# Inverse root mean square of 23 norms: GpSimd's power of -0.5 on 128x512 in place of ScalarE's root and VectorE's reciprocal

## The chip, the cores and the metric

The kernel runs on one core of a Trainium2 chip. Time is device time in microseconds (us) of one execution. The engines are TensorE (PE; PEld is its weight load), VectorE (DVE), ScalarE (ACT), GpSimd (POOL) and SyncE (SP), which issues most of the DMAs. Each engine works through its own queue in order and waits on semaphores for the others.

## What is computed

One layer of a streaming encoder on x of 2048 rows by 1024 columns: a mixer (a gated linear recurrence and a gated MLP with a position mixer) and a feed-forward block, each between two RMS norms. The norm is what the change touches:

```
def rmsnorm(x, g):
    y = x * lax.rsqrt(jnp.mean(x * x, axis=-1, keepdims=True) + EPS)
    return y * g

h = rmsnorm(x, g_mix_pre) * (1.0 + sc_m) + sh_m
z = h @ w_in                       # lru_x, lru_gate, gmlp_u, gmlp_v
y = concat([rmsnorm(y_lru, g_lru_out), rmsnorm(y_gmlp, g_gmlp_out)])
x = x + gt_m * rmsnorm(y @ w_out, g_mix_post)
h = rmsnorm(x, g_ffn_pre) * (1.0 + sc_f) + sh_f
up = causal_depthwise_conv(h @ w_up) + b
x = x + gt_f * rmsnorm((gelu(up_g) * up_v) @ w_down, g_ffn_post)
```

## The kernel before

Columns lie on the 128 partitions, rows of x on the free axis, 512 at a time: four chunks c = 0 to 3 in the mixer, two halves C = 0, 1 of 1024 rows (two parts t each) in the feed-forward block. Every float32 matrix product is made of three TensorE matmuls of split operands (hi x hi, hi x lo, lo x hi, `mm3`), 128x512 each. The split (`split`, L136 to L141) is a cast on ScalarE (or GpSimd) and a subtraction on VectorE or GpSimd, so each weight tile and each activation passes through ScalarE and VectorE before TensorE may read it. Weight tiles come from a pool of 8 (four split pairs).

A norm runs in three steps. `SumSq` squares on ScalarE and adds on GpSimd (or VectorE), `rms_split` splits the sums on VectorE, and `rms_bcast` multiplies them with a matrix of 1/D on TensorE (L199), which gives the mean square of each row on all 128 partitions, 128x512 in PSUM. Then r = 1/sqrt(mean + eps) is made in the tile `..._r`, by ScalarE (L202) and VectorE (L203). This is called 23 times, and the tiles are named by their place:

- n1, n2, n3: before the mixer, for chunks 1 to 3 (chunk 0 has code of its own, L725 and L726); read by `build_h` (L253).
- rl0 to rl3 and rg0 to rg3: the two norms in the middle of the mixer; read by `norm_scale` (L530).
- rp0 to rp3: after the mixer's last product; read by `mixer_post` (L604, chunks 0 and 1) and `late_post` (L583, chunks 2 and 3, inside the feed-forward block).
- rq0 to rq3: before the feed-forward block; read by `normed` (L851).
- fr00, fr01, fr10, fr11: after the down-projection of half C, part t; read by `final` (L1112), the last of them at the kernel's end.

In the mixer a chunk's z products (`zblock`: 24 matmuls each) run beside the output products of the chunk before (`mixer_out`: 8 blocks of 24). GpSimd has the odd weight splits (L141), the sums of squares (L219), two products of the recurrence (L380, L503), the copies of split weights to DRAM (L169) and one small power: the variance of the gated MLP's norm, 128x4 (L442). In the feed-forward block the up-projection runs over 24 blocks f; the first two of C = 0 are plain (`up_plain`, 96 matmuls each), the others are made of seven products of 12 matmuls (`up_pair`), whose weights need sums that GpSimd makes (L951, L953, L956, L959) in C = 0 and for the first two f of C = 1. The down-projection runs over 24 f with 24 matmuls each.

The order of the work on each engine is not the order of the code: a scheduler replays the program with priorities (`high_priority`) and estimated durations, and each engine's queue is fixed by it. So a change of one operation moves others too.

Of the kernel before, what the change touches and what calls it, by code (L numbers as in the profile page):

```python
# [12 lines left out]
AF = mybir.ActivationFunctionType  # L13
ALU = mybir.AluOpType

P = 128
# [24 lines left out]
def block_kernel(ctx: ExitStack, tc: tile.TileContext, xt, cols, rows, wada, wada_r, win_k, win_s, win_v, wgate, wsp, wout, wup, wdown, out):  # L41
# [12 lines left out]
    vec, act, pool, pe, sync = nc.vector, nc.scalar, nc.gpsimd, nc.tensor, nc.sync  # L54
# [15 lines left out]
    def bank(name):  # L70

        return banks[0].tile([P, 512], F32, tag="pf", name=name) if banks else psum(name)[:, 0]
# [52 lines left out]
    epst = const.tile([P, 1], F32, name="epst")  # L125
    vec.memset(epst, EPS)
    mhalf = const.tile([P, 4], F32, name="mhalf")
# [67 lines left out]
    def rms_bcast(shl, scale, name, tag="r2", bufs=2, n=512):  # L195

        pt = bank(f"{name}_m")
        for q in range(2):
            pe.matmul(out=pt[:, :n], lhsT=onesD, rhs=shl[:, q, :n], start=(q == 0), stop=(q == 1))  # L199
        r = rp.tile([P, 512], F32, tag="r", name=f"{name}_r")  # L200
        with tc.high_priority(offset=100):
            act.activation(out=r[:, :n], in_=pt[:, :n], func=AF.Sqrt, scale=scale, bias=epst)  # L202
            vec.reciprocal(out=r[:, :n], in_=r[:, :n])  # L203
        return r

    class SumSq:
# [27 lines left out]
    def x_rms(c, late=2):  # L234
        q = SumSq(f"n{c}")
        for j in range(4):
            q.add(load_x(xt, c, j, f"xq{c}"))
            yield
        yield
        hl = q.done()  # L240
        yield from wait(late)
        rx[c] = rms_bcast(hl, 1.0, f"n{c}", "rr", 4)
# [271 lines left out]
    def norm_scale(c, late=2):  # L514

        qs = []
        for tiles, name in zip(HU[c], (f"rl{c}", f"rg{c}")):
            qs.append(SumSq(name))
            for t in tiles:
                qs[-1].add(t)  # L520
            yield
        hls = [q.done() for q in qs]
        yield from wait(late)
        rs = [rms_bcast(hl, 2.0, f"r{n}{c}") for n, hl in zip("lg", hls)]
        yield
        for tiles, gname, r in zip(HU[c], ("g_lru_out", "g_gmlp_out"), rs):
            for j in range(2):
                for b in range(2):
                    t = tiles[j][:, b]
                    vec.scalar_tensor_tensor(out=t, in0=t, scalar=col(gname, 2 * j + b), in1=r, op0=ALU.mult, op1=ALU.mult)  # L530
                yield
# [37 lines left out]
    def late_rms(c, q):  # L569
        hl = q.done()  # L570
        yield
        rlate[c] = rms_bcast(hl, 1.0, f"rp{c}")
# [655 lines left out]
```

## Time and profile before

| | |
|---|---|
| Median of 3 runs | 2222.09 us (2219.21 to 2222.97) |
| The profiled execution's own time | 2222.2 us |
| Its span, first to last instruction | 2220.4 us |
| Mean granted TensorE clock | 0.971 |
| Busy: TensorE, VectorE, ScalarE, GpSimd | 2072.0, 1435.9, 928.8, 424.8 us |

The stages of the profiled execution: chunk 0 of the mixer until about 95 us, the other chunks until about 700 us, up-projection of the first half until about 1200, its down-projections until about 1460, then the same for the second half, and the end at 2220. A row of the profile names the line of the kernel, the engine, the operation, and what it writes and reads; a line can be that of a helper that many callers share, so the names of the tiles tell the place.

### The profile page before, as it was taken

What the parts mean: (1) busy time and instruction counts of PE and PEld (TensorE: products, weight loads), DVE (VectorE), ACT (ScalarE), POOL (GpSimd) and SP (SyncE); (2) the same over time, 40 slices, a digit from 0 to 9 for tenths busy, and PEclk for the clock granted to TensorE, in tenths of its full rate; (3) what the DMA queues carried; (4) which work ended last, traced back from release to release, by engine and by line L of the source; (5) the groups of instructions that cost most, each with busy time, mean ns of one, the idle gap of its engine ahead of it and who ended that gap; (6) DMA issues with size and microseconds to landing.
All of it is one profiled execution on the core that took longest, in us unless ns stands there. A gap on an engine that the chain in (4) does not pass through costs nothing.

```text
span 2220.4 us, 24098 instructions
## 1 busy us (share of the span) xinstructions
PE 2072.0 (93%) x9032; PEld 1700.7 (77%) x9032; DVE 1435.9 (65%) x1598; ACT 928.8 (42%) x1154; POOL 424.8 (19%) x248
## 2 busy tenths in 40 slices
PE   5898969999998998799999999989999999999995
PEld 4686858888877876588888888868888888888883
DVE  7788789795766887898777437474444444533634
ACT  3472733534635544355555344343233332422422
POOL 4454243234203332443320000020000000000000
PEclk9999989999999999899999999999999999999997
DMA  8587568587674887877775546537666666444541
GB/s 315 187 311 286 193 242 291 206 287 256 225 268 164 305 314 265 311 264 276 271 291 189 181 134 215 173 120 286 220 221 224 220 223 221 145 159 149 212 148 60
DMA packets 157748, 501.14 MB, mean 226 GB/s; under 512 B 15296, under 2 KB 15424, under 8 KB 157632
## 3 DMA queue, kind: packets, MB, share of 16 engines
q1 hardware_dynamic: 149568, 470.25, 59.9%
q0 software_dynamic: 6912, 25.17, 2.9%
q10 hardware_dynamic: 1152, 4.19, 0.5%
q8 instruction: 71, 1.16, 0.2%
q14 instruction: 45, 0.37, 0.1%
HBM read 343.31 MB, written 156.24 MB: 225 GB/s over the span
## 4 chain that ended last, share of the span: by engine, by line
PE 73%; DVE 14%; ACT 4%; DMA 4%; issue 4%; POOL 1%; SPq 0%; DVEq 0%; ACTq 0%; POOLq 0%
PE dn L177 8%; PE dn L178 8%; PE dn L179 8%; PE upa L973 7%; PE upa L972 7%; PE upa L971 7%; PE upc L973 3%; PE upc L972 3%; PE upc L971 3%; PE upb L973 2%; PE upb L971 2%; PE upb L972 2%; PE lg L177 1%; PE lg L178 1%; PE lg L179 1%
## 5 line engine op out<-in xcount | busy, mean ns | idle before, releaser
L177 PE MATMUL dn<-gh,wd_h 128*128 128x512 f32 x768 | 297.0, 390 | 2.9 <-ACT fr_r L202 1.6
L178 PE MATMUL dn<-gl,wd_h 128*128 128x512 f32 x768 | 296.6, 389 | 0.0
L141 DVE TENSOR_TENSOR wd_l<-wd_r,wd_h 128x1024 fp32r<-128x1024 f32 x96 | 118.0, 1230 | 231.9 <-ACT wd_h L136 216.1
L179 PE MATMUL dn<-gh,wd_l 128*128 128x512 f32 x768 | 265.0, 389 | 0.0
L136 ACT CAST wd_h<-wd_r 128x1024 fp32r<-128x1024 f32 x96 | 101.2, 1056 | 286.8 <-PE dn L178 276.1
L918 DVE SCALAR_TENSOR_TENSOR a<-Rg,prm,a 128x1023 f32<-128x1023 f32 x92 | 132.4, 1439 | 126.9 <-ACT a L916 126.7
L177 PEld LDWEIGHTS dn<-gh,wd_h 128*128 128x128 f32 x768 | 144.2, 188 | 35.4 <-ACT wd_h L136 3.0
L179 PEld LDWEIGHTS dn<-gh,wd_l 128*128 128x128 f32 x768 | 144.1, 188 | 29.8
L178 PEld LDWEIGHTS dn<-gl,wd_h 128*128 128x128 f32 x768 | 144.2, 188 | 29.8
L918 DVE SCALAR_TENSOR_TENSOR a<-Rv,prm,a 128x1023 f32<-128x1023 f32 x92 | 121.9, 1325 | 38.7 <-ACT a L916 38.5
L951 POOL TENSOR_TENSOR wt<-wuv,wug 128x512 f32<-128x512 f32 x24 | 39.3, 1637 | 523.7 <-DMA wuv<-in_wup_dram 411.7
L916 ACT ACTIVATE a<-Rv,prm 128x1024 f32<-128x1024 f32 x46 | 57.2, 1244 | 133.3 <-DVE Rv L1020 132.6
L136 ACT CAST wt<-wt 128x512 fp32r<-128x512 f32 x72 | 44.7, 622 | 113.3 <-PE upa L973 39.5
L141 DVE TENSOR_TENSOR wt<-wt,wt 128x512 fp32r<-128x512 f32 x72 | 62.7, 873 | 24.0 <-ACT wt L136 23.8
L976 ACT ACTIVATE a<-a 128x1024 f32<-128x1024 f32 x48 | 50.9, 1061 | 53.7 <-DVE a L923 31.9
L1020 DVE TENSOR_TENSOR Rv<-upa,m 128x512 f32<-128x512 f32 x46 | 31.6, 687 | 58.3 <-PE upa L973 58.3
L141 DVE TENSOR_TENSOR gl<-gr,gh 128x1024 fp32r<-128x1024 f32 x48 | 58.5, 1218 | 12.5 <-PE upa L973 6.3
L977 DVE TENSOR_TENSOR a<-a,a 128x1024 f32<-128x1024 f32 x48 | 58.8, 1225 | 2.5 <-ACT a L976 2.5
L916 ACT ACTIVATE a<-Rg,prm 128x1024 f32<-128x1024 f32 x46 | 57.2, 1243 | 4.4 <-DVE a L918 3.2
L136 ACT CAST gh<-gr 128x1024 fp32r<-128x1024 f32 x48 | 50.8, 1058 | 13.3 <-DMA gr<-gd 6.1
L1024 ACT COPY Rg<-upa 128x512 f32<-128x512 f32 x46 | 26.8, 584 | 69.7 <-PE upa L973 69.7
L959 POOL TENSOR_TENSOR wt<-wug,wt 128x512 f32<-128x512 f32 x24 | 39.9, 1662 | 82.4 <-DVE wt L141 55.5
(583 smaller groups left out, 5738.5 us busy)
## 6 DMA issues: line engine op xcount, KB each, us to landing
wd_r<-in_wdown_dram SPq DMA_DIRECT2D x96, 512.0 KB, 4.4
wkd<-wt SPq DMA_DIRECT2D x88, 512.0 KB, 4.0
wkd<-w SPq DMA_DIRECT2D x66, 512.0 KB, 3.7
w<-wkd SPq DMA_DIRECT2D x66, 512.0 KB, 4.3
gd<-a SPq DMA_DIRECT2D x48, 512.0 KB, 3.9
gr<-gd SPq DMA_DIRECT2D x48, 512.0 KB, 3.5
wrt<-wkd SPq DMA_DIRECT2D x44, 512.0 KB, 4.3
wt<-wkd SPq DMA_DIRECT2D x44, 512.0 KB, 4.6
```

The lines of the kernel that those rows point to most:

```text
L136: act.copy(out=hi, in_=src)
L141: (leng or vec).tensor_tensor(out=lo, in0=src, in1=hi.bitcast(F32), op=ALU.subtract)
L177: pe.matmul(out=out, lhsT=wh, rhs=mh, start=first, stop=False)
L178: pe.matmul(out=out, lhsT=wh, rhs=ml, start=False, stop=False)
L179: pe.matmul(out=out, lhsT=wl, rhs=mh, start=False, stop=last)
L916: act.activation(out=a, in_=R, func=AF.Identity, scale=w[2], bias=col("ffn_conv_b", blk))
L918: vec.scalar_tensor_tensor(out=a[:, s:], in0=R[:, :FT - s], scalar=w[t], in1=a[:, s:], op0=ALU.mult, op1=ALU.add)
L971: pe.matmul(out=pt, lhsT=wh, rhs=mh, start=first and not more and k == 0, stop=False, skip_group_check=more)
L972: pe.matmul(out=pt, lhsT=wh, rhs=ml, start=False, stop=False, skip_group_check=more)
L973: pe.matmul(out=pt, lhsT=wl, rhs=mh, start=False, stop=last and k == 3, skip_group_check=more)
L976: act.activation(out=g, in_=g, func=AF.Gelu_apprx_tanh)
L977: vec.tensor_tensor(out=g, in0=g, in1=v, op=ALU.mult)
```

## The change

`rms_bcast` makes r in another way. ScalarE no longer takes the root of the mean square plus eps but only adds eps (the Identity function with the same scale and bias), and leaves the sum in r in SBUF. GpSimd then raises r to the power of -0.5, in place; the exponent is the constant column `mhalf`, read with a step of zero over the 512 columns. VectorE's reciprocal is gone. All 23 calls change; the code of chunk 0 (L725, L726) keeps its root and reciprocal.

```
         with tc.high_priority(offset=100):
-            act.activation(out=r[:, :n], in_=pt[:, :n], func=AF.Sqrt, scale=scale, bias=epst)
-            vec.reciprocal(out=r[:, :n], in_=r[:, :n])
+            act.activation(out=r[:, :n], in_=pt[:, :n], func=AF.Identity, scale=scale, bias=epst)
+            pool.tensor_tensor(out=r[:, :n], in0=r[:, :n], in1=mhalf[:, 0:1].broadcast_to([P, n]), op=ALU.pow)
         return r
```

ScalarE's queue has 42 loads of a function table before and 25 after: the 11 at L202 are gone, and six on balance that served other lines.

VectorE's queue at the end of chunk 0, where n1_r is made and read (the win tiles are weight splits of chunk 1, x is the input to be scaled; - is before, + after):

```order
 L141 TENSOR_TENSOR win_10_l<-win_10_r,win_10_h 128x1024
 L444 SCALAR_TENSOR_TENSOR nm_891<-bag_879,rv_880 128x4
-L203 RECIPROCAL n_r<-n_r 128x512
+L141 TENSOR_TENSOR win_0_l<-win_0_r,win_0_h 128x1024
+L141 TENSOR_TENSOR win_2_l<-win_2_r,win_2_h 128x1024
 L253 SCALAR_TENSOR_TENSOR x_0_960<-x_0_960,sm,n_r 128x512 x2
 L253 SCALAR_TENSOR_TENSOR x_1_1007<-x_1_1007,sm,n_r 128x512 x2
```

The reciprocal is gone, two weight splits of the next chunk have moved ahead of the readers of n_r, and the readers now wait for GpSimd.

GpSimd's queue in chunk 1 (rl and rg are the two norms of chunk 0, rv the small power, xc the recurrence's input):

```order
+L219 TENSOR_TENSOR n_s_1182<-n_s_1182,n_s_1297 128x1024
 L169 DMA kept_s_1_1549<-win_5_l 128x1024
+L219 TENSOR_TENSOR n_s_1182<-n_s_1182,n_s_1352 128x1024
+L203 TENSOR_TENSOR rl_r<-rl_r,mhalf 128x512
+L203 TENSOR_TENSOR rg_r<-rg_r,mhalf 128x512
 L442 TENSOR_TENSOR rv_1696<-rv_1696,mhalf 128x4
 L380 TENSOR_TENSOR xc_0_1140<-xc_0_1140,i_0_1653 128x1024
```

Two powers stand back to back ahead of the small power and of the recurrence's product, and the sums for n2 have moved behind a weight split.

GpSimd's queue in the up-projection of C = 0 (wt_4 and wt_5 are weights of f = 4 and 5, rp_r the norm of chunk 3):

```order
 L951 TENSOR_TENSOR wt_4_5379<-wuv_4_5376,wug_4_5375 128x512
 L953 TENSOR_TENSOR wt_4_5379<-wuv_4_5376,wt_4_5379 128x512
 L956 TENSOR_TENSOR wuv_4_5376<-wuv_4_5376 128x512
-L959 TENSOR_TENSOR wt_3_5216<-wug_3_5212,wt_3_5216 128x512
 L959 TENSOR_TENSOR wt_4_5379<-wug_4_5375,wt_4_5379 128x512
+L203 TENSOR_TENSOR rp_r<-rp_r,mhalf 128x512
 L951 TENSOR_TENSOR wt_5_5552<-wuv_5_5549,wug_5_5548 128x512
```

A power stands between the weights of f = 4 and those of f = 5. In the same way rp2 stands ahead of the weights of f = 2, rq2 of f = 9 and rq3 of f = 13. On VectorE the readers of fr00 and fr10 (L1112) stand behind the weight splits of 18 blocks f of the next down-projection in the new order, where they came right after the reciprocal; those of fr01 and fr11 follow directly in both.

## Rows read from the trace of the kernel before

**Rows 1.** The page: busy time by engine, and the ended-last chain by engine.

```profile
PE 2072.0 (93%) x9032; PEld 1700.7 (77%) x9032; DVE 1435.9 (65%) x1598; ACT 928.8 (42%) x1154; POOL 424.8 (19%) x248
...
PE 73%; DVE 14%; ACT 4%; DMA 4%; issue 4%; POOL 1%; SPq 0%; DVEq 0%; ACTq 0%; POOLq 0%
```

**Rows 2.** Busy time by stretch: start:end, length, busy us of PE to POOL.

```profile
core 0: us, PE busy (x) PEld busy (x) DVE busy (x) ACT busy (x) POOL busy (x), PEclk, DMA share, GB/s
120.00:770.00 650.00, 607.04 (x2701) 500.59 (x2700) 501.61 (x529) 318.64 (x384) 221.94 (x118) 0.97 0.70 251
...
1330.00:2220.00 890.00, 849.76 (x3724) 699.27 (x3722) 430.62 (x495) 293.83 (x352) 14.66 (x8) 0.98 0.55 187
```

**Rows 3.** Lines 202 and 203: ns min/median/max; the last is L203's stretch.

```profile
L202 ACT ACT_TABLE_LOAD  x11: 1283/1283/1283, 127.2 to 2064.4; - x11
...
L203 DVE RECIPROCAL n_r<-n_r x3: 3339/3344/3352, 129.3 to 422.3; 128x512 f32<-128x512 f32 x3
...
120.00:770.00 650.00, 56.56 (x17) 0.97 0.70 251
```

**Rows 4.** Chain that ended last, in order of time: start us, us, what.

```profile
127.24 1.28 ACT L202
129.26 3.36 DVE n_r L203
...
260.88 1.22 DVE n_r L203
...
422.34 3.26 DVE n_r L203
...
427.88 3.26 DVE rq_r L203
...
1472.26 3.35 DVE fr_r L203
...
2199.47 3.36 DVE fr_r L203
```

**Rows 5.** GpSimd's plain additions: line 951 (ns min/median/max) and one of L219.

```profile
L951 POOL TENSOR_TENSOR wt<-wuv,wug x24: 1262/1661/2686, 710.0 to 1485.1; 128x512 f32<-128x512 f32 x24
...
187.19 2.40 POOL L219 TENSOR_TENSOR rg_s<-rg_s,rg_s 128x1024 f32<-128x1024 f32 x1 [1.10 <-ACT rg_s L215]
```

**Rows 6.** GpSimd's small power, line 442, and VectorE beside one of them.

```profile
L442 POOL TENSOR_TENSOR rv<-rv,mhalf x4: 1037/1192/2051, 124.8 to 539.1; 128x4 f32<-128x4 f32 x4
...
539.06 1.19 POOL L442 TENSOR_TENSOR rv<-rv,mhalf 128x4 f32<-128x4 f32 x1 [2.10 <-DVE rv L441]
...
539.40 0.69 DVE L141 TENSOR_TENSOR rq_hl<-rq_s,rq_hl 128x512 fp32r<-128x512 f32 x1
```

**Rows 7.** Timeline of the end, from the last product on.

```profile
2198.75 0.69 ACT L202 ACTIVATE fr_r<-fr_m,epst 128x512 f32<-128x512 f32 x1 [3.58 <-PE fr_m L199]
2199.47 3.35 DVE L203 RECIPROCAL fr_r<-fr_r 128x512 f32<-128x512 f32 x1 [1.61 <-ACT fr_r L202]
2202.86 5.39 DVE L1112 SCALAR_TENSOR_TENSOR fo<-fo,gf,fr_r 128x512 f32<-128x512 f32 x8
```

**Rows 8.** TensorE around its longest wait in the mixer, and the clock there.

```profile
289.10 0.39 PE L177 MATMUL o<-rg0h,wout_h 128*128 128x512 f32 x1
289.32 0.39 PE L178 MATMUL o<-rg0l,wout_h 128*128 128x512 f32 x1
...
308.94 0.77 PE L177 MATMUL o<-rl0h,wout_h 128*128 128x512 f32 x1 [18.13 <-DVE modc L285]
309.50 0.63 PE L178 MATMUL o<-rl0l,wout_h 128*128 128x512 f32 x1
309.93 0.63 PE L179 MATMUL o<-rl0h,wout_l 128*128 128x512 f32 x1
...
298.00:300.00 2.00, 0.00 (x0) 0.00 (x0) 2.00 (x4) 2.00 (x3) 0.00 (x0) 0.50 1.03 422
```

**Rows 9.** VectorE's L366 beside the addition at 187.19 us, and later alone.

```profile
187.39 2.21 DVE L366 SCALAR_TENSOR_TENSOR xc<-tails,prm,xc 128x2 f32<-128x2 f32 x1
...
193.93 0.20 DVE L366 SCALAR_TENSOR_TENSOR xc<-tails,prm,xc 128x2 f32<-128x2 f32 x1
```

## The prediction

> **What bounds the kernel now.** The first view is the page's busy time by engine: TensorE is busy for 93% of the span and VectorE for 65%, GpSimd for 19% [rows 1]. The second is the chain that ended last: 73% of it is TensorE and 14% VectorE [rows 1]. So time is lost only where TensorE stands still. The third view, busy time by stretch, says where VectorE is the next to matter: in the mixer, from 120 to 770 us, TensorE is busy for 607.0 of 650 us and VectorE for 501.6 [rows 2]; after 1330 us VectorE is busy for less than half of the time. The work that the change touches is small. The 23 reciprocals take 3.34 us each, 76.9 us of VectorE in all, and the roots bring 11 table loads of 1.283 us onto ScalarE [rows 3]. In the chain in order of time only six reciprocals stand, with 3.36, 1.22, 3.26, 3.26, 3.35 and 3.36 us, 17.8 us together, and one table load of 1.28 us [rows 4]. That is all that the removed work costs directly: 19.1 us.
>
> **What is removed.** The root becomes an Identity of the same shape on ScalarE, so its 0.69 us stays. The table loads in the order of the program fall from 42 to 25, 17 x 1.283 = 21.8 us of an engine that is busy for 42%, of which 1.28 us is on the chain. The reciprocals go from VectorE, 56.6 us of them from the mixer [rows 3].
>
> **What is added, and its price.** GpSimd gets 23 powers on 128x512, and no row shows one of that size. The nearest rows bound it from both sides. A plain two-input GpSimd operation takes 1.262 us at best on 128x512 and 2.40 on 128x1024 [rows 5], which is (2.40 - 1.262) / 512 = 2.22 ns an element and 0.12 us to start. That is the lower end: if a power costs no more than an add, p = 1.3 us. The one row with a power is that of 128x4: 1.037, 1.192 (median), 2.051 us [rows 6]. At 4 elements an add by the line above would take 0.13 us, so about 0.91 us is the power's own. If all of it is a start cost, p = 1.26 + 0.91 = 2.2 us. If all of it is paid element by element, it is 0.91 / 4 = 0.2275 us each, and p = 0.12 + 512 x 0.2275 = 117 us; from the median instead of the lowest call it would be 137. The ends are far apart. The row of the same operation is the nearer one, and with four elements it already costs seven times the addition, so I go by it. But its first call took 1.0 us more than its shortest for the same four elements, so a call has a start cost that comes and goes; I leave a third of the 0.91 us to that and take two thirds by element: 0.152 us each, p = 0.12 + 0.30 + 512 x 0.152 = **78 us**, an estimate between the ends of 1.3 and 137.
>
> [...]
>
> **Where the powers land.** Each r is read by VectorE, and VectorE and GpSimd work in order, so what stands behind is held as well. From the order of the program, shown ahead, I sort the 23.
>
> Fourteen stand in the mixer with their VectorE reader next in line: n1 to n3, the four rl, the four rg, rp0, rp1 and rq1. While VectorE waits for them, the weight splits and gate work behind it wait, and GpSimd's own share of the splits, L380 and L503 stand behind the power. What VectorE can catch up is its idle time in the mixer, 650 - 501.6 = 148.4 us, and the 17 reciprocals that it no longer runs there, 56.6 us [rows 2, 3], 205 us together. Cost: 14 x 78 - 205 = 887 us. The floor from GpSimd's own load is not far below: it is busy for 221.9 us there [rows 2], and with these fourteen, rp2 and rq0 it would have 221.9 + 16 x 78 = 1470 us of work for a stretch of 650, 820 more.
>
> Two are read with nothing between: fr01, whose reciprocal is on the chain at 1472.26 us, and fr11 at 2199.47, after which only the last scaling and the stores remain [rows 4, 7]. Each costs 78 - 3.35 = 75 us, 150 together.
>
> Three (rp3, rq2, rq3) have late readers, but on GpSimd the sums that make the up-projection's weights stand behind them (L951). TensorE has one block of f in hand, 84 matmuls at 0.227 us from start to start [rows 8], 19 us. Cost: 3 x (78 - 19) = 177 us.
>
> rp2 has the two plain blocks as cover, and rq0 one mixer_out: 192 matmuls either way, 43.6 us. Cost: 2 x (78 - 44) = 68 us.
>
> fr00 and fr10 are read 18 blocks of f later, 18 x 24 x 0.227 = 98 us: nothing.
>
> Each stall also slows TensorE's clock for a while: after the wait of 18.13 us at 308.94 the granted clock is 0.50, the level of 1.2 GHz, and ten matmuls start 0.43 us apart in place of 0.227 [rows 8], 2.0 us. Over 21 stalls, 42 us.
>
> The sum is 887 + 150 + 177 + 68 + 42 = 1324 us. Against the profiled execution's own 2222.2 us (span 2220.4, and the median of the runs is 2222.09, so no shift is needed) that is **3546 us**. For any p over 44 us the same sum reads 1908 + 21 p.
>
> **The rivals.**
>
> *The power's excess is a start cost* (p about 2.2 us). Then the six reciprocals and the table load on the chain, 19.1 us, become six powers, 13.2 us: 2216 us. If VectorE's freed 76.9 us is also felt in the mixer, up to its 43 us of TensorE idle, it could fall to 2179; I put it at 2212. This is the side of faster. The price decides: replaced one for one on the chain a power pays below 19.1 / 6 = 3.2 us, and from about 205 / 14 = 15 us on the mixer's slack is used up. For it: every other GpSimd row has a start near 0.1 us and a small slope. Against it: 0.91 us for four elements is more than any start in the trace. In this case the moved instructions also decide a few us either way; the TensorE wait of 18.13 us for the modulation [rows 8] has other blocks around it in the new order.
>
> *Everything is by element* (p = 117): 1908 + 21 x 117 = 4365 us; with p = 137 it is 4785. For it: the only row with the operation, taken as it stands. Against it: the first call's extra us.
>
> *A shorter element* (p between 18 and 45, say 30): 14 x 30 - 205 + 2 x 27 + 3 x 11 + 42 = 344, so 2566 us. It needs a loop that works on several elements at once, which four elements would not show. At p = 15 only 5 + 23 and some of the clock are left, about 2270.
>
> *The port.* A VectorE operation with two SBUF inputs is held by a GpSimd operation: L366 on 128x2 takes 0.20 us alone and 2.21 us when it starts beside an add of 2.40 us, and both end together [rows 9]. If a power holds VectorE for its whole length, it stops where nobody reads r, too: fr00 and fr10 cost 78 - 11 (two blocks of weights in hand) each, 134 us, and the covers of the five others shrink to 11, another 2 x 33 + 3 x 8 = 90: 3770 us, and 4667 with p = 117 (4365 + 2 x 106 + 90). Against it: beside the power at 539.06 a VectorE operation with two SBUF inputs ran at its usual 0.69 us [rows 6]; but four elements are read at once.
>
> The Trainium skill, SBUF — State Buffer, section Who interferes with whom, calls that pair of ports an exclusive lock, held for the whole instruction by whoever starts first. The rows of L366 agree; the row at 539.40 does not show it. By the rule the time is this rival's.
>
> **How the numbers follow.** The chance of p between 45 and 100 (2850 to 4010 us, port or not) is 0.42; of over 100 (4010 and up) 0.27; of 18 to 45 (2330 to 2850) 0.17; of 10 to 18 (2240 to 2330) 0.04; of a start cost 0.10, of which 0.07 is faster and 0.03 within 0.2%. The likeliest gives 3546 us. The range from 2330 to 4800 leaves out the start cost, the 10 to 18, and some 0.04 above for the port with p over 117, 0.18 in all. A measurement of this kernel can tell about 0.2%, 4.4 us, from no change. Faster by more: 0.07; within: 0.03; slower by more: 0.90.
>
> **What would show it.** The row of L203 on GpSimd gives p at once; GpSimd's busy time should be near 425 + 23 p, 2200 us. In the waits VectorE should wait for GpSimd's n, rl, rg, rp and rq (L253, L530, L604) for some 60 us each time, TensorE's granted clock should fall in the mixer, and the tail should grow by 75 us between the last Identity and L1112. If L203 reads under 3 us there, the first rival holds and all of the sum falls. If VectorE's two-input operations last as long as a power, the port is the better account. If p is near 78 and the time is under 3000, the cover was misjudged.

## The result

The changed kernel takes 3619.28 us (median of 4 runs, 3613.97 to 3620.29), beside 2222.53 us for the kernel before on the same chip (4 runs, 2219.21 to 2224.73). The ratio is 1.628, with a 95% interval of 1.6254 to 1.631. The profiled execution took 3619.97 us with a span of 3618.2, so its rows stand for the median.

The first view is the page of the kernel after: busy time by engine, and the chain that ended last by engine. They answer to [rows 1].

```profile
PE 2105.9 (58%) x9032; PEld 1720.8 (48%) x9032; DVE 1397.0 (39%) x1575; ACT 906.3 (25%) x1137; POOL 2296.0 (63%) x271
...
PE 30%; issue 16%; POOL 9%; POOLq 2%; DVE 2%; DMA 1%; ACT 1%; SPq 0%; DVEq 0%; ACTq 0%
```

TensorE's work is the same 9032 matmuls and only 34 us longer, but it is now 58% of the span in place of 93%. GpSimd went from 424.8 to 2296.0 us. No engine is full; the time is lost in waits between engines. The shares of the chain in this page add up to about 60%, so I read the waits and the stretches instead.

The price stands in the rows of the powers. The groups are those of line 203 and of the small power of line 442 (ns min/median/max, first and last start):

```profile
L203 POOL TENSOR_TENSOR rl_r<-rl_r,mhalf x4: 81929/81939/81950, 291.1 to 1521.8; 128x512 f32<-128x512 f32 x4
L203 POOL TENSOR_TENSOR rg_r<-rg_r,mhalf x4: 81914/81917/81936, 373.0 to 1603.7; 128x512 f32<-128x512 f32 x4
L203 POOL TENSOR_TENSOR fr_r<-fr_r,mhalf x4: 81917/81918/82545, 2551.8 to 3518.9; 128x512 f32<-128x512 f32 x4
...
L442 POOL TENSOR_TENSOR rv<-rv,mhalf x4: 999/1314/2052, 124.5 to 1399.3; 128x4 f32<-128x4 f32 x4
```

A power on 128x512 takes 81.9 us, nearly the same each time, where the reciprocal took 3.34 [rows 3].

Who waits is in the list of waits of the kernel after: engine and line, what released it, us in total, times, the longest.

```profile
DVE uu L530 <- POOL rg_r L203: 292.8, 4, 75.5
PE rp_m L199 <- DVE rp_hl L140: 287.1, 2, 144.8
DVE r L530 <- POOL rl_r L203: 280.9, 4, 79.8
PE upc L971 <- ACT wt L136: 195.9, 4, 85.0
ACT rq_s L215 <- POOL oo L605: 192.2, 7, 86.3
DVE x L253 <- POOL n_r L203: 177.7, 3, 63.1
DVE oo L604 <- POOL rp_r L203: 158.9, 2, 80.1
ACT wt L136 <- POOL wt L951: 155.3, 5, 78.4
DVE fo L1112 <- POOL fr_r L203: 150.8, 2, 83.6
```

Five of these rows are readers of r on VectorE (L530 twice, L253, L604, L1112). ScalarE's wait for L951 is of the other kind: plain additions on GpSimd that came late because a power stood ahead of them. (L605 adds to what L604 makes, so it is late with its reader.) The 195.9 us of TensorE are the end of that second chain: power, sum of weights (L951), cast on ScalarE (L136), product. TensorE's two longest waits (L199, 287.1 us) are for the split sums of squares of a later norm (rp_hl); at the second of them GpSimd makes the last of these sums at 1276.98 us, right behind the powers rl and rg.

By stretch (start:end, length, busy us and counts of PE, PEld, DVE, ACT, POOL, the granted clock) the kernel after reads as below; the cuts are the first matmul of the up-projection and the first of the down-projection.

```profile
120.00:1750.00 1630.00, 551.06 (x2320) 445.83 (x2319) 417.80 (x450) 267.78 (x320) 1452.49 (x116) 0.66 0.25 88
1750.00:2407.00 657.00, 480.39 (x2043) 392.64 (x2043) 398.70 (x440) 238.16 (x342) 448.35 (x101) 0.85 0.56 210
2407.00:3618.00 1211.00, 992.01 (x4341) 816.68 (x4339) 493.93 (x558) 352.15 (x420) 340.95 (x12) 0.91 0.48 156
```

The same cuts in the kernel before:

```profile
120.00:682.00 562.00, 519.04 (x2321) 427.92 (x2319) 433.26 (x464) 276.19 (x327) 191.17 (x102) 0.96 0.71 253
682.00:1186.00 504.00, 475.95 (x2029) 388.39 (x2030) 412.05 (x445) 249.24 (x349) 164.96 (x96) 0.97 0.75 274
1186.00:2220.00 1034.00, 993.09 (x4354) 817.59 (x4353) 504.84 (x563) 355.66 (x423) 14.66 (x8) 0.98 0.54 183
```

So 1068 of the 1398 us of span come in the mixer, 153 in the up-projection of the first half and 177 in the rest. In the mixer TensorE does the same 2320 matmuls in 551 us in place of 519: 32 us are the lower clock (0.66 granted on the mean), the rest is standing still.

The end, in the timeline of the kernel after (start, us, engine, line), answers to [rows 7]:

```profile
3518.09 0.69 ACT L202 ACTIVATE fr_r<-fr_m,epst 128x512 f32<-128x512 f32 x1 [3.58 <-PE fr_m L199]
3518.85 81.92 POOL L203 TENSOR_TENSOR fr_r<-fr_r,mhalf 128x512 f32<-128x512 f32 x1 [48.14 <-ACT fr_r L202]
3600.80 5.39 DVE L1112 SCALAR_TENSOR_TENSOR fo<-fo,gf,fr_r 128x512 f32<-128x512 f32 x8 [83.60 <-POOL fr_r L203]
```

From the start of the Identity to that of L1112 it is 82.7 us where it was 4.1: fr11 costs 78.6 us with nothing to hide it.

### The profile page after: what moved, and what is told of

Its sections match the earlier page's. It is cut to its first block, busy times and chain, and to the rows that moved or that the text cites. A ratio compares the mean times of both kernels' runs of the same rounds, so it can differ in the third digit from the quotient of the medians.

```text
span 3618.2 us, 24077 instructions
## 1 busy us (share of the span) xinstructions
PE 2105.9 (58%) x9032; PEld 1720.8 (48%) x9032; DVE 1397.0 (39%) x1575; ACT 906.3 (25%) x1137; POOL 2296.0 (63%) x271
## 4 chain that ended last, share of the span: by engine, by line
PE 30%; issue 16%; POOL 9%; POOLq 2%; DVE 2%; DMA 1%; ACT 1%; SPq 0%; DVEq 0%; ACTq 0%
POOL fr_r L203 5%; PE upa L971 4%; PE upa L972 4%; PE upa L973 4%; PE dn L177 2%; POOLq L1223 2%; POOL rg_r L203 2%; PE dn L178 2%; PE dn L179 2%; PE upc L973 2%; PE upc L971 2%; PE upc L972 2%; PE upb L971 1%; PE upb L972 1%; PE upb L973 1%
## 5 line engine op out<-in xcount | busy, mean ns | idle before, releaser
L203 POOL TENSOR_TENSOR fr_r<-fr_r,mhalf 128x512 f32<-128x512 f32 x4 | 328.3, 82074 | 812.4 <-ACT fr_r L202 812.4
L203 POOL TENSOR_TENSOR rp_r<-rp_r,mhalf 128x512 f32<-128x512 f32 x4 | 328.7, 82178 | 42.1 <-ACT rp_r L202 42.1
L203 POOL TENSOR_TENSOR rl_r<-rl_r,mhalf 128x512 f32<-128x512 f32 x4 | 327.8, 81939 | 30.0 <-ACT rl_r L202 30.0
L203 POOL TENSOR_TENSOR rq_r<-rq_r,mhalf 128x512 f32<-128x512 f32 x4 | 329.3, 82327 | 15.5 <-ACT rq_r L202 15.5
L203 POOL TENSOR_TENSOR rg_r<-rg_r,mhalf 128x512 f32<-128x512 f32 x4 | 327.7, 81921 | 0.0
L203 POOL TENSOR_TENSOR n_r<-n_r,mhalf 128x512 f32<-128x512 f32 x3 | 246.8, 82261 | 9.6 <-ACT n_r L202 9.6
L136 ACT CAST wd_h<-wd_r 128x1024 fp32r<-128x1024 f32 x96 | 101.2, 1056 | 308.8 <-PE dn L178 300.5
L177 PE MATMUL g<-xch,ghi 128*128 128x512 f32 x32 | 16.3, 508 | 266.4 <-ACT gg L409 135.5
L199 PE MATMUL rp_m<-rp_hl,onesD 128*128 128x512 f32 x8 | 3.7, 487 | 287.1 <-DVE rp_hl L140 287.1
L530 DVE SCALAR_TENSOR_TENSOR uu<-uu,prm,rg_r 128x512 f32<-128x512 f32 x16 | 27.6, 1785 | 292.8 <-POOL rg_r L203 292.8
L951 POOL TENSOR_TENSOR wt<-wuv,wug 128x512 f32<-128x512 f32 x24 | 38.3, 1599 | 159.3 <-DMA wuv<-in_wup_dram 98.9
L199 PEld LDWEIGHTS rp_m<-rp_hl,onesD 128*128 128x128 f32 x8 | 1.7, 213 | 288.1 <-issue 145.2
L177 PEld LDWEIGHTS g<-xch,ghi 128*128 128x128 f32 x32 | 7.7, 240 | 270.1 <-ACT gg L409 136.7
```

Of the source, the lines that this page charges most:

```text
L136: act.copy(out=hi, in_=src)
L177: pe.matmul(out=out, lhsT=wh, rhs=mh, start=first, stop=False)
L203: pool.tensor_tensor(out=r[:, :n], in0=r[:, :n], in1=mhalf[:, 0:1].broadcast_to([P, n]), op=ALU.pow)
L951: pool.tensor_tensor(out=t1, in0=b12, in1=b11, op=ALU.subtract)
```

## The experiments

All comparisons below are with the kernel before on the same chip (2221 to 2224 us). A time given with one number is one run. The theory of the prediction is that a power is paid by element, and that VectorE's wait for it, with what stands behind the power on GpSimd, carries the loss. The rivals were another price, GpSimd's load alone, readers alone, and the port.

**Half of the columns.** The power does 256 of the 512 columns (edit against the kernel after; three dots stand for what is left out here).

```
-            act.activation(out=r[:, :n], in_=pt[:, :n], func=AF.Identity, scale=scale, bias=epst)
-            pool.tensor_tensor(out=r[:, :n], in0=r[:, :n], ..., op=ALU.pow)
+            m = n // 2
+            act.activation(out=r[:, :m], in_=pt[:, :m], func=AF.Identity, scale=scale, bias=epst)
+            act.activation(out=r[:, m:n], in_=pt[:, m:n], func=AF.Identity, scale=0.0, bias=one)
+            pool.tensor_tensor(out=r[:, :m], in0=r[:, :m], ..., op=ALU.pow)
```

> The changed kernel with the power on the first 256 of the 512 columns alone; the other 256 are set to 1 by a second ScalarE operation (the inverse root of half of the rows is left out). By element, the power takes 256 x 0.16 = 41.0 us and the sum of the prediction for that price, 14 x 41 - 205 + 2 x 37.6 + 3 x 22 + 42, gives 552 us on top of 2222: 2774 us. If a third of the price were a start cost, the power would take 27 + 27 = 55 us and the time would be 3060 us.

It took 2771.42 us, as the price by element had it (2774). The rows of its powers:

```profile
L205 POOL TENSOR_TENSOR rg_r<-rg_r,mhalf x4: 41110/41114/41603, 291.5 to 1023.6; 128x256 f32<-128x256 f32 x4
L205 POOL TENSOR_TENSOR fr_r<-fr_r,mhalf x4: 41115/41116/41959, 1810.8 to 2711.2; 128x256 f32<-128x256 f32 x4
```

Between 256 and 512 columns the medians of rg give (81.917 - 41.114) / 256 = 0.1594 us for each column, and 81.917 - 512 x 0.1594 = 0.3 us are left as a start. The price is by element. With four elements that line gives 0.95 us, and the shortest call of L442 took 1.00: the small power lies on the same line, though one width could not tell its slope from its start.

**A product in place of the power.** The same instructions on the same engines, but GpSimd multiplies (edit against the kernel after).

```
-            act.activation(out=r[:, :n], in_=pt[:, :n], func=AF.Identity, scale=scale, bias=epst)
-            pool.tensor_tensor(out=r[:, :n], ..., op=ALU.pow)
+            act.activation(out=r[:, :n], in_=pt[:, :n], func=AF.Identity, scale=0.0, bias=one)
+            pool.tensor_tensor(out=r[:, :n], ..., op=ALU.mult)
```

> The changed kernel with the price of the power taken away and everything else kept: GpSimd multiplies the 128x512 tile by the same constant column in place of raising it to the power, and ScalarE's Identity has scale 0 and bias 1, so r is a constant and not the inverse root (that part of the computation is left out). If the price of the power (81.9 us each) is the whole of the loss, as the prediction's sum has it, the time falls to between 2185 and 2222 us, since the six reciprocals and one table load on the chain (19.1 us) become six multiplications of about 1.6 us (9.6 us). Rival: the new order of the work on the engines costs something by itself; then the time stays above 2240 us.

It took 2219.92 us (12 runs; 17 of before, 2222.08), ratio 0.9985 (0.9975 to 0.9995). The products took 1.03 to 2.7 us each. So the way over GpSimd costs nothing as long as its operation is short, and the loss comes with the price of the power. The order of the queues is not that of the change, though. Here VectorE's readers of fr00 follow right behind the product (start at 1334.8 us, the product's at 1333.1); in the change they start 86 us after the power does (2637.6 and 2551.8), behind other work and without a wait for it. The run takes away the price and the order that goes with it together; no run has that order with a cheap operation, so what the order alone costs is not shown. At the price of a product this way of making r brings some 2 us, though 19.1 us of root and reciprocal stood on the chain [rows 4].

**The power on four columns.** Each row of x needs only one power. Here the sums are made with rows on partitions, 128x4, raised there, spread over a diagonal and copied to all partitions by one more product (the eight small matmuls are left out here).

```
...
+            act.activation(out=rc, in_=pt.rearrange(...)[:, :, 0], func=AF.Identity, ..., bias=epsc)
+            pool.tensor_tensor(out=rc, in0=rc, in1=mhalf, op=ALU.pow)
+            vec.tensor_tensor(out=r..., in0=ident..., in1=rc..., op=ALU.mult)
+            pe.matmul(out=pt, lhsT=onesD.bitcast(F32), rhs=r, start=True, stop=True)
+            act.copy(out=r, in_=pt)
```

> The power on 128x4 in place of 128x512: the row sums are made with the rows on the partitions (eight small matmuls), the power takes four elements per partition, and a product of a diagonal tile with a constant matrix on TensorE spreads r over the partitions again. It computes the reference. If the price goes by the elements of one partition, the power takes about 1.0 us as in the small one of the gated MLP's norm, VectorE has 0.7 us in place of 3.34 for each norm, and the time is 2200 to 2222 us, at or a little below the kernel before. If the power has a price that does not depend on the elements, or if the longer chain of small steps is on the path 23 times (some 2 us each), the time is 2240 us or more.

It took 2254.93 us (4 runs), ratio 1.0149 (1.0136 to 1.0162). The power is cheap again (1.25 us on the mean of the 23), and 1397 us of the change's loss are down to 33. TensorE's busy time is 2114.2 us beside 2072.0: 184 more matmuls, 42 us on the engine that bounds the kernel. That accounts for the 33 by size, and TensorE's idle time did not grow (140.7 us of the span, 148.4 before), so the longer chain of small steps is not what costs; no run takes these matmuls away alone.

**Powers that nobody reads.** Root and reciprocal make r; behind them GpSimd raises a copy that ScalarE makes.

```
+            act.activation(out=r[:, :n], in_=pt[:, :n], func=AF.Sqrt, scale=scale, bias=epst)
+            vec.reciprocal(out=r[:, :n], in_=r[:, :n])
+            d = sp.tile([P, 512], F32, tag="rd", name=f"{name}_d")
+            act.activation(out=d[:, :n], in_=pt[:, :n], func=AF.Identity, ...)
+            pool.tensor_tensor(out=d[:, :n], in0=d[:, :n], ..., op=ALU.pow)
```

> ScalarE's root and VectorE's reciprocal of the kernel before make r, and the 23 powers run beside them on a tile that nobody reads. Nobody waits for a power now; only what is queued behind one on GpSimd still does. If the loss comes from readers that wait for r, the time falls to 2222 to 2320 us. If it comes from GpSimd's load (16 powers of 81.9 us and 222 us of other work in a mixer of 650 us, and the weights' sums behind rp3, rq2 and rq3), the mixer still needs some 880 us more and the up-projection some 150 to 190, and the time is 3200 to 3350 us.

It took 3490.34 us: with no reader at all, 1268 of the 1397 us are still there, more than either theory had. But the copy has one buffer, so ScalarE waited for each power before it could write the next (some 310 us in all). The next run takes that away.

**The same without ScalarE's copy.** The power reads r itself and writes the tile that nobody reads.

```
-            act.activation(out=d[:, :n], in_=pt[:, :n], func=AF.Identity, ...)
-            pool.tensor_tensor(out=d[:, :n], in0=d[:, :n], ..., op=ALU.pow)
+            pool.tensor_tensor(out=d[:, :n], in0=r[:, :n], ..., op=ALU.pow)
```

> ScalarE's root and VectorE's reciprocal make r as in the kernel before, and every reader takes that r; behind each, GpSimd raises r to -0.5 into a tile that nobody reads, and ScalarE writes nothing for it. It differs from the earlier run with unread powers in that ScalarE no longer waits for the one tile that the powers worked in. If what is queued behind the powers on GpSimd carries most of the loss, the mixer can't end before GpSimd has gone through its 16 powers and the work among them: 16 x 82 + 222 = 1534 us before the up-projection, against 682 before, so the time stays between 3050 and 3490 us. If most of the earlier run's loss was ScalarE's wait for that tile, the time falls to 2222 to 2600 us.

It took 3542.4 us, above the range given: ScalarE's wait had not been the cause. Its waits:

```profile
DVE rp_s L225 <- POOL rp_s L221: 430.7, 3, 144.5
PE rp_m L199 <- DVE rp_hl L140: 420.1, 3, 145.7
DVE rl_s L225 <- POOL rl_s L221: 212.8, 3, 79.5
```

What is late here are the sums of squares of the next norm (rp_s, rl_s; L219 of the kernel before): additions of 2.4 us that stand behind one or two powers on GpSimd. TensorE then waits for them to make the next norm.

**Only the four powers of the feed-forward's norms.**

```
+            if name[:2] == "fr":
                 (Identity and power)
+            else:
+                (root and reciprocal)
```

> Only the four powers of the feed-forward's norms (fr00, fr01, fr10, fr11) are done by GpSimd, the other 19 as before. If fr01 and fr11 each stand on the path with 82 - 3 = 79 us and fr00 and fr10 are covered, as the prediction's sum has it: 2222 + 158 = 2380 us (2365 to 2400). If only the end of the kernel waits (fr11), because fr01 is covered too: 2300 us. If all four stand on the path: 2538 us.

It took 2401.12 us, 180 above the kernel before, 21 above the sum of two powers and just outside the range given. Its first matmuls of up- and down-projection stand where they did (682.4 and 1186.5 us); all of it comes behind them. The timeline around fr01, GpSimd's rows first, then TensorE's:

```profile
1498.00 81.92 POOL L204 TENSOR_TENSOR fr_r<-fr_r,mhalf 128x512 f32<-128x512 f32 x1 [23.09 <-ACT fr_r L203]
1587.69 2.18 POOL L955 TENSOR_TENSOR wt<-wuv,wug 128x512 f32<-128x512 f32 x1 [7.78 <-DVE fo L1117]
...
1481.04 0.80 PE L975 MATMUL upa<-h_10h,w 128*128 128x512 f32 x1 [24.82 <-ACT fo L1079]
...
1505.17 0.39 PE L977 MATMUL upa<-h_11h,wt 128*128 128x512 f32 x1
1590.57 0.79 PE L975 MATMUL upc<-hs_10h,wt 128*128 128x512 f32 x1 [85.01 <-ACT wt L136]
```

At the start of the power TensorE had 7 us of products in hand. Then it waited for the power (to 1579.9), for VectorE's readers of r (the next sum of weights, L951 of the kernel before, waits 7.78 us more for fo), and for sum and cast: 85.0 us. In the kernel before, the wait at this place was 8.8 us long, behind the same readers, so fr01 costs 76:

```profile
1488.00 0.80 PE L971 MATMUL upc<-hs_10h,wt 128*128 128x512 f32 x1 [8.78 <-ACT wt L136]
```

Another 25 us come ahead of fr01's power: TensorE waits 24.8 us at 1481.04 for the first product of the second half, which came without a wait before. They go back to fr00. Its readers run at 1420.2 us in place of 1341.5, its stores follow them, and on SyncE the load of the second half's x stands behind the last of these stores. SyncE's rows before and, below the dots, in this run:

```profile
1372.62 0.38 SPq L1114 DMA_DIRECT2D out_dram<-fo  x1
1373.09 0.42 SPq L228 DMA_DIRECT2D xf<-x2d  x1
...
1452.01 0.38 SPq L1118 DMA_DIRECT2D out_dram<-fo  x1
1452.48 11.86 SPq L232 DMA_DIRECT2D xf<-x2d  x2
```

ScalarE's part in the norm of that x comes late with it, and behind it in ScalarE's queue stands the copy (L1079) that TensorE waits for. The same wait is 25.6 us long in the change. This chain is read from the trace; no run has fr00 alone. The last matmul of the up-projection starts 100 us later than before (2033.0 beside 1932.6), and the rest is the end. By this reading fr00 costs 25 us, fr01 76, fr10 nothing and fr11 79.

**Only rp2, rp3, rq2 and rq3**, the four beside the up-projection, by the same kind of condition:

```
+            if name in ("rp2", "rp3", "rq2", "rq3"):
```

> Only the four powers whose waits the prediction put beside the up-projection (rp2, rp3, rq2, rq3) are done by GpSimd, the other 19 as before. The prediction's sum has 82 - 44 = 38 us for rp2 and 82 - 19 = 63 us for each of the other three, 227 us in all: 2449 us. In the changed kernel the stretch from the first matmul of the up-projection to the first of the down-projection grew by 153 us only: 2375 us, if that holds with the mixer undisturbed. If the weights of the up-projection don't wait behind the powers at all: 2222 to 2270 us.

It took 2368.43 us, 146 above the kernel before and near the 2375 taken from the changed kernel's own stretch. The four first matmuls behind the powers (TensorE's timeline; in brackets the wait):

```profile
731.62 0.79 PE L975 MATMUL upc<-hs_00h,wt 128*128 128x512 f32 x1 [6.43 <-ACT wt L136]
852.30 0.80 PE L975 MATMUL upc<-hs_00h,wt 128*128 128x512 f32 x1 [57.91 <-ACT wt L136]
996.07 0.80 PE L975 MATMUL upc<-hs_00h,wt 128*128 128x512 f32 x1 [48.07 <-ACT wt L136]
1122.47 0.80 PE L975 MATMUL upa<-h_00h,wt 128*128 128x512 f32 x1 [49.93 <-ACT wt L136]
```

All four are waits for a weight whose sum stood behind a power, as the prediction had it, but smaller: rp2 is hidden but for 6 us, and the other three cost 52 us each on the mean.

**GpSimd for the powers alone.** All other work of GpSimd goes to VectorE, and its stores to ScalarE's queue. First with root and reciprocal, as a base:

```
-        pool.tensor_tensor(...)          # L380, L503, L605, L951, L953, L956, L959
+        vec.tensor_tensor(...)
-            self.acc, self.name, self.n, self.eng = None, name, 0, eng or pool
+            self.acc, self.name, self.n, self.eng = None, name, 0, eng or vec
-    ... weight_once(..., pool if b % 2 else vec)
+    ... weight_once(..., vec)
-            pool.dma_start(out=k, in_=t.bitcast(F32))
+            act.dma_start(out=k, in_=t.bitcast(F32))
```

> The kernel before, with all of GpSimd's additions, products, splits of weights and weight combinations handed to VectorE, and its stores of kept weights issued by ScalarE; root and reciprocal as before. It is the base for the next run. VectorE was busy for 1436 us of 2220 and takes on some 200 us, so 2222 to 2400 us by both theories.

It took 2182.06 us, below the kernel before; on that more at the end. Then with the powers, read as in the change:

> The changed kernel, with all of GpSimd's other work handed to VectorE and ScalarE as in the run beside it, so that GpSimd holds the powers and next to nothing else; each power is read as in the change. If GpSimd's own load bounds the mixer, it falls by the 222 us that were taken off it (first matmul of the up-projection from 1749 to some 1500 to 1550 us), the weights of the up-projection no longer stand behind a power, and the time is 3619 - 222 - 100 = 3300 us (3200 to 3380) plus what the base costs over 2222. If the wait of each power's reader bounds it, the first matmul of the up-projection stays within 60 us of 1749, and the time is above 3450 us.

It took 3293.5 us, 1111 above its base and in the range of the first theory. The first matmul of the up-projection is at 1594.7 us, 155 earlier than in the change (30 of them are the base's), between what the two theories had for it. The up-projection of the first half lasts 487 us, as in the base (491): no sum stands behind a power any more, and its 153 us are gone. But the wait of fr01 is still there: now L951 stands on VectorE, behind the readers of fr01. Waits of this kernel:

```profile
ACT wt L136 <- DVE wt L951: 84.4, 5, 78.0
PE upc L971 <- ACT wt L136: 86.0, 2, 84.6
```

**Powers that nothing waits for.** The same base, with 23 powers on GpSimd that take a constant and write a tile that nobody reads; nothing is queued among them.

```
             vec.reciprocal(out=r[:, :n], in_=r[:, :n])
+            pool.tensor_tensor(out=d[:, :n], in0=epst[:, 0:1].broadcast_to([P, n]), ..., op=ALU.pow)
...
-        pool.tensor_tensor(out=rv, in0=rv, in1=mhalf, op=ALU.pow)
+        act.activation(out=rv, in_=rv, func=AF.Sqrt)
+        vec.reciprocal(out=rv, in_=rv)
```

> GpSimd does the 23 powers of 128x512 and nothing else (its other work is on VectorE and ScalarE as in the run that was the base for the powers alone, the small power of 128x4 there is a root and a reciprocal); the powers take a constant, write a tile that nobody reads and wait for nothing, so they run one behind the other from the start, 23 x 82 = 1886 us, beside the whole mixer and both up-projections. If the loss is waiting alone (for the power, or for what is queued behind it), all of it goes, although GpSimd is as busy as in the change: 2180 to 2230 us. If a power also slows VectorE, by the ports or in another way, VectorE's operations with two inputs in the mixer last longer beside it and the time is above 2400 us.

It took 2192.89 us, as given for waiting alone, 11 above its base, with GpSimd at 87%. Its busy line, and three groups of VectorE's operations with two inputs in SBUF (us in all, mean ns) which ran beside powers:

```profile
PE 2061.3 (94%) x9032; PEld 1693.6 (77%) x9032; DVE 1421.8 (65%) x1791; ACT 937.9 (43%) x1165; POOL 1895.5 (87%) x30
...
L141 DVE TENSOR_TENSOR wt<-wt,wt 128x512 fp32r<-128x512 f32 x72 | 49.4, 690 | 14.5 <-ACT wt L136 14.5
L279 DVE SCALAR_TENSOR_TENSOR ada_m<-wada,cact,ada_m 128x1024 f32<-128x1024 f32 x28 | 36.0, 1284 | 14.6 <-DMA wada<-in_wada_r_dram 14.5
L607 DVE SCALAR_TENSOR_TENSOR oo<-oo,gm,rp_r 128x512 f32<-128x512 f32 x16 | 10.8, 744 | 0.0
```

The three means are within 1% of those of the base's next run below (685, 1280, 743 ns). A busy GpSimd alone costs next to nothing; the waits for it are the whole loss.

**The stages side by side**: start of the first matmul of the up-projection and of the down-projection, the span, and the three stretches against the base of each (the kernel before, for the last two the kernel with GpSimd cleared).

| Kernel | up | down | span | mixer | up-projection | rest |
|---|---|---|---|---|---|---|
| before | 681.9 | 1186.3 | 2220.4 | | | |
| after | 1749.5 | 2407.0 | 3618.2 | +1068 | +153 | +177 |
| unread, power of r | 1699.8 | 2372.6 | 3540.6 | +1018 | +168 | +134 |
| only fr | 682.4 | 1186.5 | 2399.4 | +1 | 0 | +179 |
| only rp2, rp3, rq2, rq3 | 676.5 | 1335.7 | 2366.7 | -5 | +155 | -3 |
| GpSimd cleared, old r | 652.1 | 1143.6 | 2180.2 | | | |
| GpSimd cleared, powers read | 1594.7 | 2081.7 | 3291.4 | +943 | -4 | +173 |
| GpSimd cleared, nothing waits | 661.3 | 1154.1 | 2191.1 | +9 | +1 | 0 |

In the mixer the queue alone (no readers) makes 1018 of the 1068 us, and the readers alone (on GpSimd little but powers) make 943 against their base; without both it is 9. The two don't add up: either is enough. A reason that fits the traces, but that no run tests by itself, is that both make one chain of powers of 82 us, one behind the other: the next norm needs either what the reader makes or what stood behind the power. With GpSimd cleared and the powers read, GpSimd is busy for 1272 of the 1473 us from 122.0 us to the up-projection. In the up-projection only the queue counts (-4 without it).

**A version that beats both.** The base of the last runs, timed again.

> The kernel before, with GpSimd's additions, products, splits of weights and weight combinations on VectorE and its stores of kept weights issued by ScalarE, root and reciprocal as before: the base of the run with powers alone, now timed in rounds. Its one look gave 2182 us beside 2221, so if that was no accident 2175 to 2190 us, 1.5 to 2% under the kernel before; if it was, within 0.2% of 2222 us.

It took 2180.02 us (5 runs, 2177.3 to 2185.18; 9 of before, 2222.23), ratio 0.9816 (0.9803 to 0.9829), within the range given. VectorE has 189 instructions more than in the kernel before and is busy for less: 1412.9 us in place of 1435.9. Three of its groups in this kernel (us in all, mean ns):

```profile
L141 DVE TENSOR_TENSOR wt<-wt,wt 128x512 fp32r<-128x512 f32 x72 | 49.1, 685 | 15.1 <-ACT wt L136 15.1
L277 DVE SCALAR_TENSOR_TENSOR ada_m<-wada,cact,ada_m 128x1024 f32<-128x1024 f32 x28 | 35.8, 1280 | 15.9 <-DMA wada<-in_wada_r_dram 15.9
L604 DVE SCALAR_TENSOR_TENSOR oo<-oo,gm,rp_r 128x512 f32<-128x512 f32 x16 | 10.8, 743 | 0.0
```

And the same groups in the kernel before:

```profile
L141 DVE TENSOR_TENSOR wt<-wt,wt 128x512 fp32r<-128x512 f32 x72 | 62.7, 873 | 24.0 <-ACT wt L136 23.8
L277 DVE SCALAR_TENSOR_TENSOR ada_m<-wada,cact,ada_m 128x1024 f32<-128x1024 f32 x28 | 47.1, 1682 | 7.6 <-DMA wada<-in_wada_r_dram 7.6
L604 DVE SCALAR_TENSOR_TENSOR oo<-oo,gm,rp_r 128x512 f32<-128x512 f32 x16 | 23.6, 1544 | 0.0
```

Over all groups that stand in both, VectorE's instructions became 181 us shorter (difference of the means times the count), because no GpSimd addition runs beside them: of the 72 subtractions of the first group, in the kernel before, the 23 that run at the same time as a two-input operation of GpSimd take 1.28 us on the mean, and the other 49 take 0.68. VectorE took on some 172 us of GpSimd's work for that. GpSimd's help cost VectorE as much as it saved. Of the 42 us, 33 come in the mixer and 12 in the up-projection of the first half, where GpSimd had its work (the rest is 2 us longer); which waits they were is not shown by a run.

## Why the prediction came out

The forecast of 3546 us is 73 us short of 3619. Its mechanisms hold in the main; part of the closeness is luck, and one term, fr00, was put at nothing and is not.

- **The price.** 78 us were taken, 81.9 measured. The view was right (the row of the same operation, not that of the additions), but the split of its 0.91 us was not: a third was put down to a start cost, and the runs show a line of 0.159 us an element with 0.3 us to start. Two thirds was a guess, and it was luck that the 0.152 us taken lies near 0.159; the bound of 117 us had charged the start to the elements as well. With 81.9 in place of 78 the formula, 1908 + 21 p, gives 3628, 9 us over the measured time.
- **The mixer.** At 81.9 us the fourteen give 942, rq0 38, and 15 of the 21 lost clocks 30: 1010 beside 1068 measured, 5% short. The clock was right (32 us of TensorE's busy time). The rest lies in the cover: 205 us of VectorE's idle time and freed reciprocals were counted as wholly usable. How much of them was used isn't shown by any run. What the sum named as the cause, VectorE's reader next in line, is only half of it: the floor by GpSimd's own load, the powers and the work among them, which the sum put at 820 us "not far below", does as much by itself (1018 with nobody reading).
- **The up-projection.** Three weights at 63 and rp2 at 38 give 227; alone they cost 146. The mechanism was right (all four are sums of weights behind a power), the cover was mis-sized: not 19 us of products in hand but some 30, since 52 of 82 are left, and for rp2 some 75, since its power starts 39 us before the up-projection does.
- **fr01 and fr11.** 79 each at 81.9, and right: fr11 is 78.6 and fr01 76. That fr01's loss stays when L951 moves to VectorE shows that either queue is enough to hold it.
- **fr00 and fr10 at nothing.** Right for fr10, wrong for fr00, which costs 25 us. The step took the 98 us of down-projections as cover for a power of 82, but behind the late readers stand their stores, and behind these the load of the second half's x.
- **The removed work.** It was put at 19.1 us on the chain; with a product in its place, and the order that goes with that, it is worth some 2 us. ScalarE lost 22.5 us of busy time (928.8 to 906.3), as 17 table loads would give. The first rival's 2212 us would have been too low even at its own price, since products of 1.03 to 2.7 us gave 2219.9.
- **The port.** It fell. In the kernel after, VectorE's subtraction of 128x1024 beside fr00's power lasts as long as anywhere:

```profile
2551.78 82.55 POOL L203 TENSOR_TENSOR fr_r<-fr_r,mhalf 128x512 f32<-128x512 f32 x1 [166.91 <-ACT fr_r L202]
...
2559.46 1.23 DVE L141 TENSOR_TENSOR wd_l<-wd_r,wd_h 128x1024 fp32r<-128x1024 f32 x1 [1.22 <-ACT wd_h L136]
2566.85 1.22 DVE L141 TENSOR_TENSOR gl<-gr,gh 128x1024 fp32r<-128x1024 f32 x1
```

At 81.9 us, with 2 us of clock for each stall, the sum is 58 us short in the mixer, 82 over in the up-projection and 16 short behind it (161 beside 177, for want of fr00). These errors nearly cancel, so that the total is better than its terms: that is luck. The run with half of the columns (2774 expected, 2771 measured) hides the same: its sum has some 400 us in the mixer and 74 in the up-projection, where its trace has 446 and 31.

## What to carry to other kernels

Price an operation on GpSimd from a row of that operation, however small its tile, and take it by element until a second width says otherwise; the rows of other operations on the same engine said 1.3 us where it was 82. A slow instruction in an in-order queue charges everything behind it, so count who reads it and who is queued behind it as two ways to the same loss, not as two terms to be added; and follow a late reader on to its stores and to the loads behind them. And look at what GpSimd's plain additions do to VectorE's rows: work handed to GpSimd to relieve VectorE can lengthen VectorE's own instructions by as much.

## What the hardware showed that was not expected

- A GpSimd power is paid by the element: 1.0 us at 4, 41.1 at 256, 81.9 at 512 columns, 0.159 us for each. A product of the same shape took 1.03 us at best, 80 times less. The Trainium skill, GPSIMD Engine Reference, section 3.1 (side-by-side cycle accounting), has some 2.6 cycles an element of two-input operations; by an estimate from that figure, at the section's 1.2 GHz, 512 elements are 1.1 us. The product agrees; the power doesn't.
- A power of 82 us doesn't hold VectorE's two-input operations (1.22 us beside it, 690 ns on the mean where the base had 685), while additions on GpSimd do (1.28 us on the mean beside one, 0.68 without, and L366 in [rows 9]). The Trainium skill, SBUF — State Buffer, section Who interferes with whom, has one rule for both: the ports that the two engines share are an exclusive lock, and a VectorE instruction with two SBUF inputs contends with a GpSimd instruction that reads SBUF. The additions agree with it, the power doesn't. Why the two differ is not shown here.
- 23 powers beside the whole kernel, 1886 us of them, cost 11 us as long as nothing waits (one run of each kernel); how much of that is due to the four roots and reciprocals that took the place of the small powers is not shown.
